# Table matmuls that write every fourth word of a PSUM bank

## The chip, the cores and the metric

The kernel runs on one core of a Trainium2 chip. The metric is the device time of one execution in microseconds. Before the change three runs gave 1797.10, 1792.04 and 1797.41 us, median 1797.1.

## The reference

One layer of a streaming encoder, 512 tokens of 1024 features, all in float32: a chunked attention and an mLSTM with gates, and behind them a layer of very many single-neuron experts (PEER). The change touches the last one:

```
q = (xb @ w_pq).reshape(PEER_BLOCK, PEER_HEADS, 2, D_KEY // 2)
s = jnp.einsum("thpd,hpnd->thpn", q, sub_keys)
s_top, i_top = lax.top_k(s, PEER_TOPK)
...
e = i1 * N_KEYS + i2
gate = jax.nn.softmax(best, axis=-1)
act = jax.nn.gelu(jnp.einsum("thkd,td->thk", u_exp[e], xb))
return jnp.einsum("thk,thkd->td", gate * act, v_exp[e])
```

Every token picks 16 experts for each of 8 heads, 128 in all, out of 128 x 128, by two keys i1 and i2, and each has a gate.

## The kernel before, in words

128 tokens get their experts by gathering rows from HBM. For the other 384 the kernel computes all 16384 experts densely, 128 at a time, and multiplies each activation by a table of gates, which is zero where the token did not pick the expert.

The stages follow each other: mixers and projections up to about 500 us, the selection of experts (`scores`, `select`) to about 700 us, the table build (`build`) from 702 to 868 us, the dense experts (`output`, with the gather of the 128 tokens woven in) to the end. Beside selection and build runs `ahead`, which computes the first 40 of the 128 groups of hidden activations (`hidden`: 24 matmuls into `ps_act`, with the u rows loaded on the SP queue and split by ACT, DVE and POOL into a high and a low part). Its pace beside the build is 0.15 of a group for each step of `build`.

The table of a token t has an entry for every pair (i1, i2). It is the product of two one-hot matrices: `oa` has, for each of the token's 128 slots (partitions), the gate in the column of i2; `o4` has a one in the column of i1, for four tokens at once. One matmul for each token, 128x128 by 128x128 in float32, gives the table (L766); the profile shows each such matmul as two records. Four tokens fill a bank of PSUM (128 partitions x 512 words). ACT then copies the bank into the block `st` in SBUF (L767), which holds 32 tokens as [partition][i1][token]: the 32 tokens of one i1 lie side by side. A block is full after eight banks, and POOL's queue writes it to HBM with one DMA of 2 MB (L772). There are 12 blocks, so 96 banks and 96 copies.

Who makes the operands: DVE `o4` (L750), one per bank; of the four `oa` of a bank, DVE makes two, POOL one (L764), and ACT one by two operations (L760, L761). Banks for `ps_g` come from the tags g and w, two each; `st` has two buffers, so one is filled while the other is written out.

Each engine has a queue of its own and waits on semaphores, which the builder places from the reads and writes of the tiles. The order inside a queue is planned by the builder, which simulates the program's timeline (L1024): the loops issue the 24 matmuls of a group of `ahead` in a row, and the trace shows them interleaved with table matmuls. Behind the stage, `output` loads v rows (`vst`) and table blocks (`gq`) on the SP queue and gathers on POOL's.

The lines of this text: L766 table matmul, L767 copy, L772 block's DMA, L750/760/761/764 operands, L163 to L165 the three matmuls of a split product (`ps_act` in `hidden`, `acc` in `output`), L150 and L153 the split, L135 the loads.

Of the kernel before, what the change touches and what calls it, by code (L numbers as in the profile page):

```python
# [21 lines left out]
P = 128  # L22
# [58 lines left out]
def tile_block(  # L81
# [17 lines left out]
    stop=None,  # L99
):  # L100
    nc = tc.nc
# [8 lines left out]
    def bank(tag, name):  # L110
        return psum.tile([P, 512], F32, tag=tag, name=name, bufs=4 if tag == "acc" else 2)
# [623 lines left out]
    def build(cp, i, slots):  # L735

        ps = bank("g", "ps_slT")
        for j in range(3):
            nc.tensor.transpose(ps[:, j * P : (j + 1) * P], slots[:, j].rearrange("p h k -> p (h k)"), ident)
        sT = cp.tile([P, 3, P], F32, tag="sT", name="sT", bufs=2)  # L740
        nc.scalar.copy(sT, ps[:, : 3 * P].rearrange("p (j t) -> p j t", j=3))
        neg = cp.tile([P, 2, P], F32, tag="neg", name="neg", bufs=2)
        nc.scalar.mul(neg, sT[:, 1:, :], -1.0)
        for b in range(P // TB):
            st = cp.tile([P, P, TB], F32, tag="gst", name="gst", bufs=2)
            for t4 in range(TB // 4):
                ps = bank("gw"[t4 % 2], "ps_g")
                o4 = cp.tile([P, 4, P], F32, tag="two", name="o4", bufs=TWO)
                t0 = b * TB + t4 * 4
                mark = nc.vector.tensor_tensor(  # L750
                    out=o4, in0=iota.unsqueeze(1).broadcast_to([P, 4, P]),
                    in1=sT[:, 0, t0 : t0 + 4].unsqueeze(2).broadcast_to([P, 4, P]), op=ALU.is_equal,
                )
                for tt in range(4):
                    t = b * TB + t4 * 4 + tt
                    oa = cp.tile([P, P], F32, tag="oap" if tt == 1 else "oad", name="oa", bufs=OAP if tt == 1 else OAD)
                    at = sT[:, 1, t : t + 1]
                    gt = sT[:, 2, t : t + 1]
                    if tt == 0 and t4 % ACT_D < ACT_N:
                        nc.scalar.activation(oa, iota, AF.Abs, bias=neg[:, 0, t : t + 1])  # L760
                        nc.scalar.activation(oa, oa, AF.Relu, scale=neg[:, 1, t : t + 1], bias=gt)  # L761
                    else:
                        e = nc.gpsimd if tt == 1 else nc.vector
                        e.tensor_scalar(oa, iota, at, gt, op0=ALU.is_equal, op1=ALU.mult)  # L764
                    ob = o4[:, tt]
                    nc.tensor.matmul(ps[:, tt * P : (tt + 1) * P], oa, ob, start=True, stop=True)  # L766
                nc.scalar.copy(  # L767
                    st[:, :, t4 * 4 : t4 * 4 + 4].rearrange("p i t -> p t i"),
                    ps.rearrange("p (t i) -> p t i", t=4),
                )  # L770
                yield
            nc.gpsimd.dma_start(gd[i * (P // TB) + b], st)  # L772
            state.setdefault("marks", []).append(mark.ins)
# [6 lines left out]
    def front(sp, dp, h2T):  # L780
        yield from scores(sp, h2T)
        for i in range(NG, 4):
            yield from build(dp, i, state["slots"][:, i])
# [244 lines left out]
```

## Time and profile before

| what | before |
|---|---|
| median of three runs | 1797.1 us (1792.04 to 1797.41) |
| profiled execution | 1789.01 us |
| its span, first to last instruction | 1787.2 us |
| PE busy | 1711.7 us (96%) |
| DVE busy | 1372.9 us (77%) |
| ACT busy | 841.5 us (47%) |
| POOL busy | 824.8 us (46%) |
| copies L767, all 96 | 104.8 us, mean 1129 ns |
| table matmuls L766, 768 records | 103.4 us |

PE, DVE, ACT, POOL and SP are the engines; PEld is PE's loading of weights. Times in the views are microseconds from the first instruction, those marked ns excepted. Instructions of one engine overlap at their ends, so that the time from start to start of two in a row tells better than a duration how long one holds the engine. The ends of matmuls are modelled.

### The profile page before, as it was taken

To read this page: it belongs to the slowest core of one execution; us is meant where nothing else is said; L and a number is where in the kernel's file an instruction comes from. 1 tells how busy PE (TensorE), PEld (TensorE's weight loads), DVE (VectorE), ACT (ScalarE), POOL (GpSimd) and SP (SyncE) were. 2 spreads that over 40 slices of the span, in tenths; PEclk is the share of its full clock that TensorE was granted. 3 is DMA by queue.
4 is the path that set the end of the run, shared out by engine and by line. 5 is a ranking of instruction groups with operands and counts; after the bars stand their busy time and mean duration, and the time that the engine had idled before them with its cause. 6 is when DMAs were issued, how large, how long until landed. Compare 5 with 4: busy or idle time off the path is not lost.

```text
span 1787.2 us, 25467 instructions
## 1 busy us (share of the span) xinstructions
PE 1711.7 (96%) x8671; PEld 1483.7 (83%) x8671; DVE 1372.9 (77%) x2868; ACT 841.5 (47%) x1624; POOL 824.8 (46%) x692
## 2 busy tenths in 40 slices
PE   5999999999899988999999999999999999999997
PEld 4766678888798777888889999999999999998886
DVE  7557656674599998788277988989898998898445
ACT  5544545444533326999643343434443334334443
POOL 0000000000267677788446666677766777673221
PEclk9999999999999999999999999999999999999999
DMA  8424234553222333545799999989999989988653
GB/s 298 151 66 142 77 107 141 205 196 118 96 95 89 117 106 126 218 195 212 294 375 322 345 314 353 338 316 340 352 343 342 349 312 356 335 294 294 217 201 106
DMA packets 129940, 413.35 MB, mean 231 GB/s; under 512 B 12049, under 2 KB 38801, under 8 KB 128274
## 3 DMA queue, kind: packets, MB, share of 16 engines
q1 hardware_dynamic: 91218, 252.33, 41.0%
q0 software_dynamic: 38592, 159.40, 23.8%
q8 instruction: 68, 1.11, 0.2%
q14 instruction: 62, 0.51, 0.1%
HBM read 376.03 MB, written 35.66 MB: 230 GB/s over the span
## 4 chain that ended last, share of the span: by engine, by line
PE 79%; DVE 9%; ACT 7%; DMA 2%; issue 2%; POOL 1%; SPq 0%; DVEq 0%; ACTq 0%; POOLq 0%
PE acc L165 10%; PE acc L163 10%; PE acc L164 10%; PE ps_act L165 8%; PE ps_act L163 8%; PE ps_act L164 8%; ACT gst L767 4%; DVE wlo L153 1%; ACT oa L761 1%; PE ps_ya L361 1%; PE ps_s L341 1%; PE ps_pq L165 1%; PE ps_pq L163 1%; PE ps_pq L164 1%; PE ps_qk L163 1%
## 5 line engine op out<-in xcount | busy, mean ns | idle before, releaser
L150 ACT CAST whi<-wst 128x512 fp32r<-128x512 f32 x408 | 253.1, 623 | 479.4 <-PE ps_act L164 277.0
L165 PE MATMUL ps_act<-h2T_hi,wlo 128*128 128x384 f32 x1024 | 347.5, 339 | 7.2 <-DVE wlo L153 6.1
L163 PE MATMUL ps_act<-h2T_hi,whi 128*128 128x384 f32 x1024 | 346.5, 338 | 0.0
L164 PE MATMUL ps_act<-h2T_lo,whi 128*128 128x384 f32 x1024 | 346.1, 338 | 0.0
L164 PE MATMUL acc<-wlo,ehi 128*128 128x512 f32 x768 | 299.1, 391 | 0.0
L163 PE MATMUL acc<-whi,ehi 128*128 128x512 f32 x768 | 293.4, 390 | 5.8 <-ACT whi L150 5.8
L153 DVE TENSOR_TENSOR wlo<-wst,whi 128x512 fp32r<-128x512 f32 x275 | 206.9, 755 | 109.8 <-ACT whi L150 103.8
L165 PE MATMUL acc<-whi,elo 128*128 128x512 f32 x768 | 286.9, 391 | 0.0
L153 POOL TENSOR_TENSOR wlo<-wst,whi 128x512 fp32r<-128x512 f32 x133 | 184.6, 1394 | 192.5 <-ACT whi L150 185.8
L150 ACT CAST whi<-vst 128x512 fp32r<-128x512 f32 x256 | 158.0, 620 | 180.9 <-PE acc L165 143.3
L710 POOL DMA_INDIRECT ur<-in_u_r,ei x128 | 153.6, 1200 | 115.1 <-DVE junk L713 95.2
L153 POOL TENSOR_TENSOR wlo<-vst,whi 128x512 fp32r<-128x512 f32 x85 | 132.9, 1564 | 155.2 <-ACT whi L150 139.8
L724 POOL DMA_INDIRECT vr<-in_v_r,ei x128 | 163.6, 1278 | 86.9 <-DVE sum_v L730 68.7
L165 PEld LDWEIGHTS ps_act<-h2T_hi,wlo 128*128 128x128 f32 x1024 | 193.3, 189 | 10.2 <-DVE wlo L153 8.0
L163 PEld LDWEIGHTS ps_act<-h2T_hi,whi 128*128 128x128 f32 x1024 | 193.4, 189 | 3.8
L164 PEld LDWEIGHTS ps_act<-h2T_lo,whi 128*128 128x128 f32 x1024 | 193.4, 189 | 3.8
L730 DVE SCALAR_TENSOR_TENSOR sum_v<-vr,act,sum_v 128x1024 f32<-128x1024 f32 x127 | 180.3, 1420 | 1.6 <-DMA vr<-in_v_r,ei 0.8
L163 PEld LDWEIGHTS acc<-whi,ehi 128*128 128x128 f32 x768 | 144.5, 188 | 34.3 <-ACT whi L150 6.1
L713 DVE SCALAR_TENSOR_TENSOR junk<-ur,h 128x1024 bf16<-128x1024 f32 x128 | 170.9, 1335 | 0.9
L165 PEld LDWEIGHTS acc<-whi,elo 128*128 128x128 f32 x768 | 144.1, 188 | 30.6 <-DVE elo L841 0.5
L164 PEld LDWEIGHTS acc<-wlo,ehi 128*128 128x128 f32 x768 | 144.1, 188 | 28.4
L153 DVE TENSOR_TENSOR wlo<-vst,whi 128x512 fp32r<-128x512 f32 x171 | 132.5, 776 | 28.1 <-ACT whi L150 27.4
(300 smaller groups left out, 3018.9 us busy)
## 6 DMA issues: line engine op xcount, KB each, us to landing
wst<-in_u_t SPq DMA_DIRECT2D x128, 512.0 KB
vst<-in_v_e SPq DMA_DIRECT2D x128, 512.0 KB
wst<-in_w_pieces SPq DMA_DIRECT2D x76, 512.0 KB
wst<-in_w_ada SPq DMA_DIRECT2D x48, 512.0 KB
gd<-gst POOLq DMA_DIRECT2D x12, 2048.0 KB
gq<-gd SPq DMA_DIRECT2D x16, 1536.0 KB
ad<-gelu SPq DMA_DIRECT2D x8, 768.0 KB
aq<-ad SPq DMA_DIRECT2D x8, 768.0 KB
```

The costliest lines, as they stand in the source:

```text
L150: nc.scalar.copy(hi, t[:, cs])
L153: e.tensor_tensor(out=lo, in0=t[:, cs], in1=hi.bitcast(F32), op=ALU.subtract)
L163: nc.tensor.matmul(o, a[0], b[0], start=first, stop=False)
L164: nc.tensor.matmul(o, a[0], b[1], start=False, stop=False)
L165: return nc.tensor.matmul(o, a[1], b[0], start=False, stop=last)
L341: nc.tensor.matmul(pss[:, :n], qaT[po : po + 64, cs], kaT[po : po + 64, hp, :n], start=True, stop=True)
L361: nc.tensor.matmul(psy[po : po + 64, cs], va[:, kt, h * 64 : (h + 1) * 64], pt[:, kt * P : (kt + 1) * P], start=kt == 0, stop=kt == qt,)
L710: nc.gpsimd.indirect_dma_start(out=t, out_offset=None, in_=u_r, in_offset=bass.IndirectOffsetOnAxis(ap=ei[:, j : j + 1], axis=0))
L713: nc.vector.scalar_tensor_tensor(junk(), t, 1.0, state["h2"][i], op0=ALU.mult, op1=ALU.mult, accum_out=act[:, j : j + 1])
L724: nc.gpsimd.indirect_dma_start(out=t, out_offset=None, in_=v_r, in_offset=bass.IndirectOffsetOnAxis(ap=ei[:, j : j + 1], axis=0))
L730: nc.vector.scalar_tensor_tensor(sum_v, t, act[:, j : j + 1], sum_v, op0=ALU.mult, op1=ALU.add)
L767: nc.scalar.copy(st[:, :, t4 * 4 : t4 * 4 + 4].rearrange("p i t -> p t i"), ps.rearrange("p (t i) -> p t i", t=4),)
```

## The change

The matmul of the tt-th token of a bank no longer writes words 128 tt to 128 tt + 127, but words tt, tt + 4, tt + 8 and so on. So the bank holds [i1][token] in place of [token][i1]. The copy reads its 512 words in order, as it did before. Its writes come in another order: before, 128 single words, 32 words apart, for each token in turn; now runs of four neighbouring words (four tokens of one i1), the runs 32 words apart. What stands in `st` in the end is the same.

```
                     ob = o4[:, tt]
-                    nc.tensor.matmul(ps[:, tt * P : (tt + 1) * P], oa, ob, start=True, stop=True)
+                    nc.tensor.matmul(ps[:, tt::4], oa, ob, start=True, stop=True)
                 nc.scalar.copy(
-                    st[:, :, t4 * 4 : t4 * 4 + 4].rearrange("p i t -> p t i"),
-                    ps.rearrange("p (t i) -> p t i", t=4),
+                    st[:, :, t4 * 4 : t4 * 4 + 4],
+                    ps.rearrange("p (i t) -> p i t", t=4),
                 )
```

## Rows read from the trace of the kernel before

**Rows 1.** The page, first part: busy time, share of the span and instructions of each engine.

```profile
PE 1711.7 (96%) x8671; PEld 1483.7 (83%) x8671; DVE 1372.9 (77%) x2868; ACT 841.5 (47%) x1624; POOL 824.8 (46%) x692
```

**Rows 2.** The page, second part: busy tenths in 40 slices of 44.7 us, DMA engines alike.

```profile
PE   5999999999899988999999999999999999999997
...
ACT  5544545444533326999643343434443334334443
...
DMA  8424234553222333545799999989999989988653
```

**Rows 3.** Windows: stretch, its length, busy us of each engine, clock, DMA share, GB/s.

```profile
702.00:868.00 166.00, 155.91 (x1104) 145.05 (x1104) 127.15 (x288) 164.96 (x323) 132.53 (x124) 1.00 0.52 203
868.00:880.00 12.00, 12.00 (x72) 12.00 (x71) 2.97 (x5) 5.45 (x12) 3.19 (x3) 1.00 1.01 368
880.00:900.00 20.00, 14.22 (x73) 13.61 (x73) 6.45 (x12) 7.13 (x14) 8.59 (x9) 0.83 1.01 366
900.00:1600.00 700.00, 700.00 (x3534) 636.44 (x3533) 614.21 (x768) 278.46 (x506) 473.24 (x359) 1.00 0.93 336
```

**Rows 4.** Chain of waits from 702 to 868 us, summed by line.

```profile
by line: ACT gst L767 43.2%; ACT oa L761 13.1%; ACT oa L760 8.9%; PE ps_g L766 7.2%; ACT whi L150 5.5%; POOL oa L764 4.2%; issue 3.8%; PE ps_act L165 3.0%; PE ps_act L164 2.9%; PE ps_act L163 2.8%; POOL wlo L153 2.7%; ACT gelu L790 2.2%; PE
```

**Rows 5.** Groups by line and shape, 702 to 868 us; columns as in the page's fifth part.

```profile
L767 ACT COPY gst<-ps_g 128x512 f32<-128x512 f32 x96 | 104.8, 1129 | 0.0
L766 PE MATMUL ps_g<-o,oa 128*128 128x128 f32 x768 | 103.4, 281 | 10.1 <-ACT gst L767 4.1 <-ACT oa L761 3.5 <-POOL oa L764 2.2
L764 POOL TENSOR_SCALAR oa<-iota,sT 128x128 f32<-128x128 f32 x94 | 100.1, 1076 | 2.3 <-PE ps_g L766 1.7
...
L163 PE MATMUL ps_act<-h2T_hi,whi 128*128 128x384 f32 x110 | 38.2, 347 | 0.0
```

**Rows 6.** Timeline of ACT from 802.92 us: start, length, instruction.

```profile
802.92 1.14 ACT L767 COPY gst<-ps_g 128x512 f32<-128x512 f32 x1
803.80 0.45 ACT L760 ACTIVATE oa<-iota,neg 128x128 f32<-128x128 f32 x1
804.09 1.10 ACT L767 COPY gst<-ps_g 128x512 f32<-128x512 f32 x1
804.93 0.54 ACT L761 ACTIVATE oa<-oa,sT,neg 128x128 f32<-128x128 f32 x1
```

**Rows 7.** Timeline of ACT at 615.51 us, in the selection stage.

```profile
615.51 0.59 ACT L627 COPY sc<-ps_sc 128x512 f32<-128x512 f32 x1 [0.50 <-PE ps_sc L625]
615.99 0.59 ACT L621 COPY pqT<-ps_pq 128x512 f32<-128x512 f32 x1
```

**Rows 8.** Timeline of PE from 771.00 us, one round of the build stage.

```profile
771.00 1.05 PE L766 MATMUL ps_g<-o,oa 128*128 128x128 f32 x8
771.81 0.42 PE L164 MATMUL ps_act<-h2T_lo,whi 128*128 128x384 f32 x1
772.07 0.34 PE L165 MATMUL ps_act<-h2T_hi,wlo 128*128 128x384 f32 x1
772.24 1.05 PE L766 MATMUL ps_g<-o,oa 128*128 128x128 f32 x8
```

**Rows 9.** Timeline of PE at 1000.22 us, in the expert stage.

```profile
1000.22 0.39 PE L163 MATMUL acc<-whi,ehi 128*128 128x512 f32 x1
1000.45 0.40 PE L164 MATMUL acc<-wlo,ehi 128*128 128x512 f32 x1
```

**Rows 10.** Waits from 702 to 868 us: who waited for whom, total, times, longest.

```profile
PEld ps_g L766 <- ACT gst L767: 9.6, 24, 0.6
...
POOL gd L772 <- ACT gst L767: 6.7, 2, 4.0
```

**Rows 11.** Hand-over: timeline of SP, chain of waits, timeline of PE.

```profile
878.62 0.33 SPq L135 DMA_DIRECT2D wst<-in_u_t  x1
...
879.68 16.25 DMA vst<-in_v_e
...
896.68 1.65 PE L163 MATMUL acc<-whi,ehi 128*128 128x512 f32 x3 [5.78 <-ACT whi L150]
```

## The prediction

> **What bounds the kernel now.** The page's engine line comes first: PE is busy for 96% of the span, nobody else for more than 77% [rows 1]. That is an average over stages, so the slices come next: ACT stands at 2 to 6 tenths nearly everywhere and at 9 only in three slices of 44.7 us, the seventeenth to the nineteenth [rows 2]. They lie in the table build, which the change edits. Cut to its time, 702 to 868 us, the windows show ACT busy for 164.96 of 166 us, PE for 155.91, POOL for 132.53, DVE for 127.15, the DMA engines at 0.52 of their time [rows 3]. The chain of waits of the stretch says the same from the other side: 43.2% of it is the copy of L767, 22.0% the two ACT operations of L760 and L761, 7.2% the table matmuls [rows 4]. So in this stage ACT sets the pace, with the copy as its largest part. In the rest of the span PE does: from 900 to 1600 us it is busy for 700.00 of 700 us [rows 3].
>
> PE's 155.91 us are too many to serve as its need, since the ends of pipelined matmuls are modelled. I take start-to-start times. In a steady stretch one round of eight table records and two ps_act matmuls lasts 772.24 - 771.00 = 1.24 us [rows 8]. Inside it the second ps_act holds PE for 772.24 - 772.07 = 0.17 us; the first ps_act of a round starts early and holds 0.09 us more, so I count both at 0.174 and the eight records at (1.24 - 0.35) / 8 = 0.112 us each. The stage has 768 records (two to each of the 384 matmuls of L766) and 3 x 110 ps_act matmuls [rows 5]. PE's need is 768 x 0.112 + 330 x 0.174 = 86.0 + 57.4 = 143.4, with six small transposes 144 us. That leaves 166 - 144 = 22 us in which PE stands still, in pieces mostly too short for the busy time to show.
>
> **The copy.** The 96 copies stay 96, with the same 512 words each in and out. What changes is the order of the writes: now consecutive words land 32 words apart in the block, afterwards four words lie side by side. Two copies, each with another ACT operation queued right behind it, hold ACT for 803.80 - 802.92 = 0.88 and 804.93 - 804.09 = 0.84 us [rows 6]; I take 0.85. An ordinary copy of 128x512 from PSUM into consecutive words, again with the next one queued, holds it for 615.99 - 615.51 = 0.48 us [rows 7]. The source of both is read in order, so the 0.37 us between them belong to the scattered writes. The trace has no copy with runs of four. Its bounds are 0.48 us (all of the penalty goes) and 0.85 us (none does, because every run still ends in a jump); below 0.48 nothing speaks for it, since the number of words is the same as in the fastest row. I take 0.48, the row nearer in kind: three of four steps are between neighbours. That takes 96 x 0.37 = 35.5 us off ACT, which then needs 165 - 35.5 = 129.5 us of the stage.
>
> **The table matmuls.** Count, operands and array time stay. Each record writes 128 words 16 bytes apart instead of 128 neighbours. No matmul of the trace writes so. A lower bound is 0.112 us, as now; a scattered write can save the array nothing. For the upper bound I borrow the only scattered write that the trace has, that of the copy, which costs 0.85 / 0.48 = 1.77 times the ordered one: 0.112 x 1.77 = 0.198 us. I take 0.112, for this reason: the fp32r matmuls of the later stage write 512 columns every 1000.45 - 1000.22 = 0.23 us, 2.2 columns per ns [rows 9], and the table records only 128 in 0.112 us, 1.14 columns per ns. The write side is asked for half of what it is seen to deliver, so a scattered write may cost up to twice an ordered one before a record becomes longer.
>
> The Trainium skill speaks against this choice: its page "PSUM — Partial Sum Buffer", section "Specifications (TRN2)", says that PSUM's lines hold two fp32 values and that an output pattern that isn't contiguous slows matmuls considerably, without a figure. No row here shows it; by that rule the run goes the way of the first rival below, 1841 us, and by the sentence above it the way of the forecast, 1781 us.
>
> **The sum.** Once ACT needs 129.5 us, PE with 144 is the next in line, then POOL with 132.5 and DVE with 127. The gain cannot be 35.5 us: it ends where PE runs without a gap, 22 us. It will not reach that. ACT alone was 15% above the next engine and reached 99% busy; PE would be only 9% above POOL, and the two feed each other in short steps (one POOL row of L764 per four matmuls, 1.08 us each [rows 5]). Some waits of the stage vanish with the slow copy: the weight load of the records waited 9.6 us for gst in 24 pieces, and POOL stood for 6.7 us at the block's DMA because the last copy was late [rows 10]; while POOL stands there, the next block's rows queue behind it. I take PE at 96% of its time, a stage of 150 us, a gain of 16 us. Nothing is added to any queue; the order of work may be planned anew, because the builder simulates the program, and rows 8 (eight and two in turn, where the loops issue 24 ps_act in a row) show that it does interleave. I count that as part of a spread of the gain from 8 to 22 us.
>
> Behind the stage the gain has to survive. At 880 to 900 us PE stands for 5.78 us, waiting for the first v rows, whose transfer takes from 879.68 for 16.25 us with the DMA engines at 1.01 [rows 3, 11]. That transfer is issued right behind the last u rows, which go out at 878.62 us [rows 11], so it moves forward with the stage. Afterwards PE has no gap for 700 us [rows 3], so an earlier start is an earlier end.
>
> The profiled execution has a span of 1787.2 us and took 1789.0; by the sum it would take 1773. The median of the runs shown is 1797.1, some 8 us above it, and the forecast stands against that: 1797.1 - 16 = **1781 us**.
>
> **Rivals.** *The matmuls pay for the scattered write.* Place: PE in the build stage. For it: PE is already the second engine of the stage, and ACT shows that jumps cost this chip something [rows 6, 7]. Against it: the half rate above [rows 9]. At 0.198 us a record PE needs 768 x 0.198 + 58 = 210 us, the stage grows by 44 us, and the run takes 1841 us. It decides from the point where PE's need passes the 166 us of today: (166 - 58) / 768 = 0.141 us a record, 26% over now. *Half of it.* At 0.123 to 0.165 us PE needs 152 to 185 us; the result lies between 8 us faster, with some waits left, and 19 us slower: 1789 to 1816 us. *The copy gets no faster.* If each jump counts and not its length, runs of four might still hold ACT for 0.85 us: ACT stays the bound, 1797 us. That the change doesn't do what it says is this case. Against it is that three jumps of four disappear. *The gain is given back at the hand-over.* The DMA engines are full from 868 to 900 us; if the v rows could not come sooner, PE would only wait longer than 5.78 us: 1797 us. Against it is the share of 0.52 in the stage [rows 3], which leaves room for what has to be moved before.
>
> **How the numbers follow.** The forecast has 0.58, the rival of the slow matmuls 0.18, its half form 0.11, the copy that stays slow 0.08, the hand-over 0.05. The forecast's own range is 1770 to 1789 us: a gain of 8 to 22 us, and 5 us more at the lower end because the runs shown begin at 1792 us. The range for 8 in 10 reaches to 1815 us, over the copy, the hand-over and the half form; outside are the slow matmuls and 0.02 below. A change of under 0.3%, 5.4 us, cannot be told from none. Faster: 0.55 of the forecast and 0.04 of the half form, 0.59. The same: 0.07 of the slow copy, 0.04 of the hand-over, 0.03 of the forecast, 0.02 of the half form, 0.16. Slower: the slow matmuls with 0.18, 0.05 of the half form, 0.02 of the two cases without an effect, 0.25.
>
> **What would show it.** The copy's row: mean near 0.6 us in place of 1.13, start to start near 0.48. The record's: a round of eight and two still 1.24 us. The build stage 14 to 22 us shorter, its chain led by PE and no longer by L767, ACT at 8 to 9 tenths. The 5.78 us wait before the first acc matmul unchanged. The prediction is wrong if a record takes more than 0.14 us start to start, or if a copy still holds ACT for more than 0.7 us: then ACT saves under 15 us, and with ACT still ahead of PE the gain is smaller than that.

## The result, and the profile after

Four runs gave a median of 1768.0 us (1767.1 to 1768.8) against 1795.6 us for the kernel before (1792.0 to 1797.4, four runs). The ratio is 0.9865, interval 0.9847 to 0.9883: of the 1789.0 us of the profiled execution before, 24 us less, between 21 and 27. The profiled execution of the changed kernel took 1767.1 us, span 1765.3, which is 21.9 us less than before. The forecast was 16 us.

The page of the changed kernel: the line of the engines, and the slices of PE and ACT.

```profile
PE 1705.3 (97%) x8671; PEld 1486.5 (84%) x8671; DVE 1380.5 (78%) x2868; ACT 806.3 (46%) x1624; POOL 832.6 (47%) x692
...
PE   5999999999999897999999999999999999999997
...
ACT  4544545443543334998533443433434443434443
```

ACT has given back 35 us of busy time (841.5 to 806.3), as much as the forecast took off it; of its three nines of [rows 2] two are left, over a shorter stage. Where the gain lies is read from the copies: the view of L767 gives the start of the first and of the last. First before, then after (columns: least, median and greatest length in ns, then the two starts).

```profile
L767 ACT COPY gst<-ps_g x96: 1017/1114/1327, 704.5 to 866.9; 128x512 f32<-128x512 f32 x96
```

```profile
L767 ACT COPY gst<-ps_g x96: 565/586/630, 706.5 to 846.4; 128x512 f32<-128x512 f32 x96
```

162.4 us have become 139.9. The first copy starts 2.0 us later than before, and from the last copy to the end it is 918.9 us instead of 920.3: 2.0 - 22.5 - 1.4 = -21.9 us. So the stage's 22.5 us are the whole gain. The windows of the changed kernel, with the stage in the first line (columns as in [rows 3]):

```profile
704.00:848.50 144.50, 144.13 (x1102) 143.64 (x1102) 133.68 (x289) 131.17 (x324) 136.48 (x125) 1.00 0.61 236
...
861.00:881.00 20.00, 16.73 (x83) 15.67 (x83) 8.79 (x16) 8.05 (x16) 9.65 (x9) 0.91 0.99 368
900.00:1580.00 680.00, 680.00 (x3439) 619.02 (x3438) 602.65 (x747) 272.45 (x494) 467.84 (x352) 1.00 0.93 335
```

PE is busy for 144.13 of 144.50 us, where it was for 155.91 of 166 [rows 3]; ACT for 131.17, where it was full. Since the ends of matmuls are modelled, the starts are the better measure: between the first and the last table matmul lie 768 records and 309 ps_act matmuls, at 0.112 and 0.174 us 139.8 us of work, and the stretch takes 141.3 us, where it took 162.4 before. The chain of waits of the stage has changed hands:

```profile
by line: PE ps_g L766 48.0%; PE ps_act L163 11.1%; PE ps_act L164 11.0%; PE ps_act L165 11.0%; POOL oa L764 8.1%; DMA gd<-gst 6.2%; POOL wlo L153 1.7%; issue 1.5%; PE ps_slT L739 0.5%; POOL gd L772 0.4%; ACT oa L760 0.3%; ACT oa L761 0.3%; 
```

In [rows 4] the copy held 43.2% and the table matmuls 7.2%; now these hold 48.0%, the ps_act matmuls 33.1%, and L767 doesn't appear. The two lines of the change, by group, answer to [rows 5]:

```profile
L766 PE MATMUL ps_g<-o,oa 128*128 128x128 f32 x768 | 94.6, 275 | 0.4 <-ACT oa L761 0.4
...
L767 ACT COPY gst<-ps_g 128x512 f32<-128x512 f32 x96 | 56.1, 590 | 11.5 <-DMA gd<-gst 6.2 <-PE ps_g L766 5.3
```

The copy's mean has gone from 1129 to 590 ns. How long it holds ACT is read from two starts in a row, as in [rows 6]; the timeline of ACT:

```profile
721.99 0.61 ACT L767 COPY gst<-ps_g 128x512 f32<-128x512 f32 x1
722.45 0.45 ACT L760 ACTIVATE oa<-iota,neg 128x128 f32<-128x128 f32 x1
```

722.45 - 721.99 = 0.46 us, against 0.84 to 0.88 before and 0.48 for the copy into consecutive words [rows 7]. A round of PE, as in [rows 8]:

```profile
760.25 1.05 PE L766 MATMUL ps_g<-o,oa 128*128 128x128 f32 x8
761.05 0.42 PE L165 MATMUL ps_act<-h2T_hi,wlo 128*128 128x384 f32 x1
761.31 0.34 PE L163 MATMUL ps_act<-h2T_hi,whi 128*128 128x384 f32 x1
761.49 1.05 PE L766 MATMUL ps_g<-o,oa 128*128 128x128 f32 x8
```

761.49 - 760.25 = 1.24 us, to the hundredth what it was: the scattered matmuls cost nothing here. Two waits of the stage:

```profile
POOL gd L772 <- ACT gst L767: 6.9, 3, 3.4
ACT gst L767 <- DMA gd<-gst: 6.2, 4, 2.4
```

The first was there before, with 6.7 us [rows 10]; the prediction let it vanish with the slow copy, and it didn't. With it POOL, busy for 136.48 us, has 143.4 of the 144.5 us taken, nearly as much as PE. The second is new: at four places the copies fill a block before the DMA has emptied the other one. It is 6.2% of the chain, but PE's work leaves only 1.5 us of its stretch free. The last view is the hand-over, chain and PE, as in [rows 11]:

```profile
860.51 13.74 DMA vst<-in_v_e
```

```profile
875.00 1.46 PE L163 MATMUL acc<-whi,ehi 128*128 128x512 f32 x3 [3.27 <-ACT whi L150]
```

PE stands for 3.27 us instead of 5.78. The stage's gain reached the end of the run.

### The profile page after: what moved, and what is told of

Its sections match the earlier page's. It is cut to its first block, busy times and chain, and to the rows that moved or that the text cites. A ratio compares the mean times of both kernels' runs of the same rounds, so it can differ in the third digit from the quotient of the medians.

```text
span 1765.3 us, 25467 instructions
## 1 busy us (share of the span) xinstructions
PE 1705.3 (97%) x8671; PEld 1486.5 (84%) x8671; DVE 1380.5 (78%) x2868; ACT 806.3 (46%) x1624; POOL 832.6 (47%) x692
## 4 chain that ended last, share of the span: by engine, by line
PE 80%; DVE 13%; DMA 4%; issue 1%; POOL 1%; ACT 1%; SPq 0%; DVEq 0%; ACTq 0%
PE acc L165 10%; PE acc L164 10%; PE acc L163 10%; PE ps_act L165 8%; PE ps_act L163 8%; PE ps_act L164 8%; PE ps_g L766 4%; DVE wlo L153 2%; DMA wst<-in_w_ada 1%; PE ps_ya L361 1%; PE ps_s L341 1%; PE ps_qk L163 1%; DVE i L648 1%; PE ps_qk L165 1%; DVE sc L649 1%
## 5 line engine op out<-in xcount | busy, mean ns | idle before, releaser
L153 DVE TENSOR_TENSOR wlo<-wst,whi 128x512 fp32r<-128x512 f32 x275 | 207.0, 756 | 98.2 <-ACT whi L150 91.1
L153 POOL TENSOR_TENSOR wlo<-wst,whi 128x512 fp32r<-128x512 f32 x133 | 184.4, 1393 | 180.9 <-ACT whi L150 174.9
L724 POOL DMA_INDIRECT vr<-in_v_r,ei x128 | 168.6, 1317 | 84.5 <-DVE sum_v L730 65.9
L153 POOL TENSOR_TENSOR wlo<-vst,whi 128x512 fp32r<-128x512 f32 x85 | 131.0, 1541 | 151.7 <-ACT whi L150 136.1
L471 POOL TENSOR_SCALAR_AFFINE_SELECT mbd<-mbc 128x512 f32<-128x512 f32 x4 | 4.7, 1163 | 319.5 <-ACT mbc L469 319.5
```

The lines of the kernel that those rows point to most:

```text
L153: e.tensor_tensor(out=lo, in0=t[:, cs], in1=hi.bitcast(F32), op=ALU.subtract)
L724: nc.gpsimd.indirect_dma_start(out=t, out_offset=None, in_=v_r, in_offset=bass.IndirectOffsetOnAxis(ap=ei[:, j : j + 1], axis=0))
```

## Experiments

The theory: the copy was dear by the order of its writes alone; ACT's sum of work bounded the stage; PE's sum bounds it now. Code is shortened: a pattern in quotes stands for the tile's rearrange. All comparisons are with runs of the kernel before on the same chip.

**One half of the change at a time.** The first kernel has the matmuls of the change and the copy's old order (against the changed kernel):

```
 matmul(ps[:, tt::4], oa, ob, ...)
-copy(st[:, :, t4 * 4 : t4 * 4 + 4], ps "p (i t) -> p i t")
+copy(st[...] "p i t -> p t i", ps "p (i t) -> p t i")
```

> The matmuls write every fourth word as in the changed kernel, but the copy writes as before, single words 32 apart, token by token; it therefore reads every fourth word of the bank. Theory (the order of the copy's writes is the whole price, the scattered matmul costs nothing): the copy holds ACT for about 0.85 us again, a table record 0.112 us, ACT is the bound of the build stage, which is back at about 164 us, and the time is within 4 us of the kernel before. Rival (the layout of the bank is what helps, the copy gains by reading it so): the copy is near 0.47 us and the time near that of the changed kernel, some 24 us below before. Third possibility: reading every fourth word costs something of its own; then the copy goes above 0.85 us, by 96 x the excess slower than before.

Ratio 1.0012, interval 0.9998 to 1.0025 (median 1793.9 against 1789.7 us): no gain. Timeline of its ACT:

```profile
721.85 1.08 ACT L767 COPY gst<-ps_g 128x512 f32<-128x512 f32 x1
722.69 0.42 ACT L760 ACTIVATE oa<-iota,neg 128x128 f32<-128x128 f32 x1
```

722.69 - 721.85 = 0.84 us, as before, although the copy now reads every fourth word of the bank: these reads cost nothing. On the scattered matmul this run says little, since ACT sets the pace and PE has time to spare.

The second has the old matmuls and the new order of the copy (against the kernel before):

```
 matmul(ps[:, tt * P : (tt + 1) * P], oa, ob, ...)
-copy(st[...] "p i t -> p t i", ps "p (t i) -> p t i")
+copy(st[:, :, t4 * 4 : t4 * 4 + 4], ps "p (t i) -> p i t")
```

> The matmuls write as before, 128 words in a row for each token; the copy writes runs of four as in the changed kernel and so reads the bank with steps of 128 words. Theory: only the writes count, the copy holds ACT for about 0.47 us, the build stage lasts about 141 us, and the time is that of the changed kernel, about 24 us below before (ratio 0.986). Rival (reads out of order cost as much as writes do): the copy stays at 0.8 us or more and the time within 4 us of before. Between them: a copy of about 0.6 us would still leave ACT, at 142 us, level with PE's 144, so that nearly the whole gain would stay.

Ratio 0.9860, interval 0.9834 to 0.9885: the whole gain. Timeline of its ACT:

```profile
722.18 0.60 ACT L767 COPY gst<-ps_g 128x512 f32<-128x512 f32 x1
722.65 0.44 ACT L760 ACTIVATE oa<-iota,neg 128x128 f32<-128x128 f32 x1
```

722.65 - 722.18 = 0.47 us, with reads that step by 128 words. Its stage, with all matmuls writing in a row:

```profile
L767 ACT COPY gst<-ps_g x96: 565/586/622, 706.7 to 846.4; 128x512 f32<-128x512 f32 x96
```

139.7 us from the first start to the last, against 139.9 with scattered matmuls: where PE has no time to spare, the scattering of 384 matmuls makes a difference of 0.2 us. So the edit of the matmul, on which the prediction spent its first rival, was not needed: the gain sits in the order in which the copy writes to SBUF.

**How many neighbours.** The changed kernel with runs of two: `st[...] "p i (a t) -> p a i t"`, t = 2, and the bank read alike.

> As the changed kernel, but the copy writes runs of two words: 256 jumps in place of 128 (changed) or 512 (before). Theory A, each jump has one price: between 0.85 us with 512 and 0.465 us with 128 jumps that is 1.0 ns a jump, so 0.59 us a copy. Theory B, a word is dear only when no neighbour follows it: 0.465 us as with runs of four. ACT needs 141 us by A and 129 us by B, both under PE's 144, so the time is about that of the changed kernel by either (A may lose up to 5 us by ACT and PE being level); the copy's start-to-start time tells them apart.

Ratio 0.9870, interval 0.9844 to 0.9896, level with the change. Its ACT:

```profile
724.38 0.66 ACT L767 COPY gst<-ps_g 128x512 f32<-128x512 f32 x1
724.87 0.46 ACT L760 ACTIVATE oa<-iota,neg 128x128 f32<-128x128 f32 x1
```

It holds ACT for 724.87 - 724.38 = 0.49 us. Of 0.38 us between single words and runs of four, pairs give back 0.35. A price for each jump (0.59 us) is refuted, and "a word is dear only without a neighbour" is nearly right. The Trainium skill, page "SBUF — State Buffer", section "Specifications (TRN2)", says that a line has 16 bytes and that full bandwidth needs at least two accesses to a line; this run agrees, within 0.03 us a copy.

**What a scattered matmul costs at full rate.** The prediction took the scattered writes for free because a table record asks for half of the columns per ns that PE is seen to deliver. 128 bf16 matmuls behind the last one test this, in one execution; their result is not used.

```
shapes = [(pr, pb), (pr "p (i t) -> p t i", pb ...), (pr "p (i a t) -> p a i t", pb ...), (pr, pb)]
for po, rhs in shapes: 32 x matmul(po, pb[:, :P], rhs)
```

> The changed kernel with 128 extra matmuls behind the last one, bf16, 128x128 by 128x512, whose result nobody reads: 32 that write 512 words in a row, 32 that write them four words apart in four passes over the bank, 32 in pairs of two, 32 in a row again. They ask the write side for about 2.2 columns per ns, twice what a table record asks for. The reason given in the prediction (a scattered write is free at half rate and may cost up to twice at full rate): the ordered ones take about 0.22 us start to start, those four apart more than that, up to 0.45 us. Rival (a scattered write costs nothing at any rate): all four groups alike, 0.22 us. If the pairs are at 0.22 us and the single words above, two neighbours are enough.

Windows of 6 us in the first, second and third group, of these instructions alone (busy time of PE and of the loading of weights, with counts):

```profile
1759.00:1765.00 6.00, 6.00 (x29) 2.73 (x28) 1.00 0.43 165
1767.00:1773.00 6.00, 6.00 (x15) 1.95 (x14) 1.00 0.05 18
...
1780.00:1786.00 6.00, 6.00 (x30) 2.73 (x28) 1.00 0.00 0
```

In the same time 28 weight loads (one to a matmul) for words in a row, 14 for words four apart, 28 for pairs. Start to start the medians are 0.216, 0.429 and 0.216 us, at a granted clock of 1.00: a scattered write costs twice an ordered one at full rate, to within 1%, and a pair nothing. That fits the reason of the prediction: scattered writes still take 512 / 0.429 = 1.19 columns per ns, and a table record asks for 1.14. It is not shown on fp32 matmuls, which might write in another way; none here asks for more. The page "PSUM — Partial Sum Buffer" of the Trainium skill (section "Specifications (TRN2)"), by which an output pattern that isn't contiguous slows matmuls, agrees with the single words at 512 columns of bf16; the pairs, and the fp32 table records, whose round kept its 1.24 us, were not slowed, and there the measurement decides.

**Less work for ACT by another way.** Instead of a faster copy, ACT makes an operand only for every other bank, DVE the other 48: `ACT_N, ACT_D = 2, 2` becomes `1, 2`, first in the kernel before, then in the changed one. The builder plans the order of work anew for both.

> The kernel before, with its slow copy, but ACT makes an operand only for every other bank; DVE makes the other 48. That takes 48 x (0.385 + 0.29) = 32 us off ACT in the build stage and puts 48 x 0.26 = 12 us on DVE (127 to 139 us busy). Theory (only ACT's load counted, and PE with its 144 us takes over): the stage shrinks from 164 to about 143 us and the run gains 20 to 24 us, as much as the change, without touching the copy. Rival (the slow copy costs by its length in the round trip bank, copy, bank, not by ACT's load): the copy keeps its 0.85 us and the gain stays under 8 us. Another: DVE becomes the bound; then the stage is about 150 us and the gain 14 us.

Ratio 0.9920, interval 0.9903 to 0.9937: 14 us, with the slow copy. The stage in one window:

```profile
708.00:855.00 147.00, 139.58 (x1044) 135.00 (x1043) 134.99 (x328) 135.82 (x225) 137.40 (x121) 1.00 0.54 212
```

It shrank from about 164 to 146 us between the first copy and the end of the last. That the copy's own length is what matters is refuted: it still holds ACT for 0.86 us. But PE is not full: DVE, ACT and POOL are all at 135 to 137 us. The gain is that of the third expectation, though not by its cause, DVE. POOL is the one without a pause: besides its 137.40 us it stands at the block's DMA until the last copy is done,

```profile
POOL gd L772 <- ACT gst L767: 9.0, 3, 4.8
```

together 146.4 of 147 us, and its rows of L764 and L153 are 36% of the chain. The new plan also left 39 ps_act matmuls fewer between the first and the last table matmul (270, not 309).

> The changed kernel with the same shift of 48 operands from ACT to DVE. Theory (PE bounds the stage, ACT is free for 15% of it): no gain, within 3 us of the changed kernel; ACT's busy time in the stage falls from 131 to about 100 us and changes nothing. If DVE at 139 to 146 us comes level with PE, it may lose up to 4 us. Rival (ACT still sets the pace somewhere in the stage): a further gain of 4 us or more.

Ratio 0.9908, interval 0.9891 to 0.9924: 5 to 8 us above the change (by the medians, 1773.6 to 1768.0, and by the ratios), and the intervals lie apart. The stage, and the longest wait of PE's weight loads in it:

```profile
701.00:842.00 141.00, 136.21 (x1035) 133.46 (x1034) 134.95 (x326) 102.81 (x224) 136.78 (x119) 1.00 0.56 220
```

```profile
PEld ps_g L766 <- POOL oa L764: 7.0, 11, 1.6
```

ACT is down to 102.81 us, and nothing is gained: it was no longer the bound. The stage itself has not grown:

```profile
L767 ACT COPY gst<-ps_g x96: 563/585/623, 701.3 to 841.4; 128x512 f32<-128x512 f32 x96
```

```profile
POOL gd L772 <- ACT gst L767: 3.3, 2, 1.9
```

140.1 us from the first start to the last, as in the changed kernel (139.9), although PE has 39 ps_act matmuls less to do in it here too. POOL holds it there, with 136.78 and 3.3 of 141 us. The matmuls left out come behind the stage, 39 x 0.174 = 6.8 us, which is about the loss. So, as far as this kernel tells, PE and POOL end the gain of the change at nearly the same place.

**How close may the next engine come.** The mis-sized step was that PE, with ACT and POOL near, would lose 4% to gaps. The first try gave ACT 11 us more by copying every fourth bank twice (`if t4 % 4 == 0:` a second `copy` behind the first).

> The changed kernel with the copy of every fourth bank done twice: 24 x 0.465 = 11 us more for ACT, which then needs about 141 us, 2% under PE's 144. It tests the step of the prediction that was mis-sized: that an engine 9% above the next one loses 4% of its time to gaps. By that step ACT this close must cost PE several per cent: 6 us or more above the changed kernel. By the other view (four banks and the operands' buffers take up the short waits, and only the largest sum counts): within 3 us of the changed kernel.

Ratio 1.0009, interval 0.9999 to 1.0019: the whole gain is gone, more than either side expected. The windows, and the copies:

```profile
704.00:752.00 48.00, 48.00 (x367) 48.00 (x366) 45.20 (x92) 44.57 (x108) 43.81 (x41) 1.00 0.58 226
752.00:800.00 48.00, 48.00 (x353) 47.97 (x351) 42.99 (x92) 44.67 (x110) 45.24 (x39) 1.00 0.58 216
...
880.00:900.00 20.00, 4.33 (x15) 3.50 (x13) 9.46 (x16) 1.24 (x2) 12.98 (x10) 0.66 1.04 396
```

```profile
L767 ACT COPY gst<-ps_g x96: 566/597/674, 706.9 to 860.5; 128x512 f32<-128x512 f32 x96
```

PE is full to 800 us and nearly so to 848 (46.79 of 48). The last copy still comes 14 us later than in the changed kernel, because the extra copies made the builder plan another order: 365 instead of 309 ps_act matmuls stand between the first and the last table matmul, 56 x 0.174 = 9.7 us more for PE. That is work done earlier, not lost. Most of what is lost comes at 880 to 900 us, where PE is busy for 4.33 us and waits for the first v rows:

```profile
PE acc L163 <- ACT whi L150: 14.2, 1, 14.2
```

In that order, besides, six gathers of u rows stand on POOL's queue ahead of the last block's DMA (issued at 865.83 us; 847.32 in the changed kernel). The next kernel lets the gathers wait for that DMA:

```
-state.setdefault("marks", []).append(mark.ins)
+state.setdefault("marks", []).append(sent.ins)     # sent: the block's dma_start
```

> The kernel with every fourth bank's copy done twice lost 24 us, nearly all behind the build stage: the plan had put six gathers of u rows on POOL's queue ahead of the last block's DMA, the table blocks and v rows came late, and PE stood for 14 us. Here the gathers wait until the last block's DMA is issued. If that order was the cause, the wait of PE for the first v rows falls to 3 to 6 us and the run comes down by 10 us or more, to within 12 us of the changed kernel. If ACT's extra 11 us were the cause, the run stays near 1791 us.

Ratio 0.9980, interval 0.9968 to 0.9993, 5 us better than without, but half of what was expected (its runs spread from 1780 to 1793 us, and the profiled one is the fastest), and the wait stayed:

```profile
PE acc L163 <- ACT whi L150: 12.8, 1, 12.8
```

So the order on POOL's queue was a part only. The chain of this kernel shows what PE waits for, and the waits of the SP queue, first without and then with the change to the gathers, show the same in both:

```profile
858.74 9.59 DMA gd<-gst
868.58 21.80 DMA gq<-gd
```

```profile
SPq L828 <- DMA gd<-gst: 7.9, 1, 7.9
```

```profile
SPq L828 <- DMA gd<-gst: 6.9, 1, 6.9
```

The load of the first table block (`gq`) stands on the SP queue ahead of the v rows and waits there for the last block's DMA, so a late last copy holds up the v rows too. In the changed kernel the queue has no such wait. Behind it the first transfers are slow: 21.34 us for the v rows without the change to the gathers and 21.80 us for the table block with it, where the first v rows of the changed kernel took 13.74. A kernel that puts the v rows ahead was not run.

The second try keeps the order of work: the copy of every fourth, or second, bank writes in the old order (`out4` and `in4` are its output and input).

```
+if t4 % 4 == 0:        # slow_half: t4 % 2 == 0
+    out4, in4 = (a.rearrange("p i t -> p t i") for a in (out4, in4))
 nc.scalar.copy(out4, in4)
```

> The changed kernel with the order of work kept, but the copy of every fourth bank writes as before, single words: 24 x (0.85 - 0.465) = 9 us more for ACT, which needs about 139 us then, 4% under PE's 144. By the prediction's step (an engine 9% above the next one loses 4% of its time) ACT this close costs 6 us or more over the changed kernel. By the view that short waits are taken up by the buffers and only the largest sum counts: within 3 us of the changed kernel, with PE busy for over 99% of the stage.

Ratio 0.9866, interval 0.9841 to 0.9890: the same as the change. The window, which holds the whole stage, and the copies:

```profile
704.00:852.00 148.00, 147.62 (x1124) 147.16 (x1123) 137.94 (x296) 142.28 (x331) 138.84 (x127) 1.00 0.60 232
```

```profile
L770 ACT COPY gst<-ps_g x96: 569/609/1162, 709.1 to 849.1; 128x512 f32<-128x512 f32 x96
```

PE 147.62 of 148 us with ACT at 142.28. Within 4% of PE, ACT costs it nothing.

> The same with every second bank: 48 x 0.385 = 18 us more, ACT needs about 148 us, 3% over PE. By the largest sum the stage is 4 to 6 us longer than in the changed kernel (from 140.5 us between the first and the last copy to some 145 or 147), and the run with it; before the change, with 165 us for ACT, it is 23 us. By the prediction's step, two engines level, it is 8 us or more.

Ratio 0.9889, interval 0.9863 to 0.9916, 1773.0 us: 4 to 5 us above the change; the intervals overlap, so the stage has to tell, again by window and copies.

```profile
704.00:852.00 148.00, 146.24 (x1099) 143.48 (x1098) 132.93 (x288) 146.94 (x323) 134.33 (x124) 1.00 0.59 228
```

```profile
L770 ACT COPY gst<-ps_g x96: 557/942/1279, 706.2 to 851.0; 128x512 f32<-128x512 f32 x96
```

Now ACT is full (146.94) and PE has gaps (146.24, by modelled ends). From the first copy to the end of the last it is 145.5 us, against 140.5 in the changed kernel and 163.6 before. With ACT needing 130, 139, 148 and 165 us the stage takes 140.5, 140.5, 145.5 and 163.6: the larger of PE's sum and ACT's, to within 4 us, and no loss where these two come near.

**Less work for PE.** The table operands in fp32r, so that a table matmul is one record; the gates of the dense experts are rounded by it. Matmuls write in a row, the copy runs of four: `F32` becomes `F32R` in the tiles `o4` and `oa`.

> Matmuls write in order and the copy writes runs of four, but the table's two operands are fp32r, so that each table matmul is one record instead of two; the gates of the dense experts are rounded to fp32r by it. PE's need in the stage falls by 384 x 0.112 = 43 us to about 101 us, if a record stays at 0.112 us or less. Theory (the largest engine's sum sets the stage): the next are DVE (134 us busy), POOL (136) and ACT (131), so the stage ends at about 135 to 140 us and the run gains 4 to 9 us over the changed kernel, not 43. But the u groups that run beside the build are paced by the order of work, so PE time freed here is used only if these groups move up. Rival: PE is the only thing that counts, and the run gains 30 us or more.

Ratio 0.9991, interval 0.9981 to 1.0000: no gain at all.

```profile
704.00:752.00 48.00, 44.43 (x288) 43.27 (x287) 48.00 (x78) 42.42 (x104) 47.54 (x43) 1.00 0.60 221
752.00:800.00 48.00, 45.67 (x297) 45.42 (x297) 46.49 (x85) 43.55 (x106) 42.52 (x38) 1.00 0.68 254
800.00:848.00 48.00, 39.49 (x146) 33.52 (x146) 46.07 (x122) 41.47 (x105) 43.06 (x39) 0.53 0.54 214
...
880.00:900.00 20.00, 4.00 (x11) 3.49 (x12) 11.16 (x22) 2.60 (x6) 10.54 (x8) 0.61 1.04 395
```

```profile
PE acc L163 <- ACT whi L150: 12.5, 1, 12.5
PE ps_g L766 <- DVE oa L764: 6.0, 6, 2.1
```

DVE is full (48.00 of 48) or nearly, as expected, so PE's saved records cannot be used. Three things went beyond that. The stage takes 150.9 us from the first copy to the end of the last, not 135 to 140; this plan, too, has 365 ps_act matmuls in it, with their splits on DVE and POOL, and whether that is all stays open. In the last of three windows of 48 us, from 800 to 848 us, the granted clock is 0.53, nearly all of the time the lower level of 1.2 GHz: this order has used up the ps_act matmuls earlier (175, 190 and 0 in the three windows), and PE stood between table matmuls for their operands. And at 880 to 900 us PE shows the same stand as above, 12.5 us for the first v rows, again under an order planned anew and with the SP queue waiting 5.1 us for the last block's DMA.

## Why the prediction was right, and which step was mis-sized

**The bound.** Right. ACT's load set the stage: 35 us less by fast copies, or 18 of them given back by slow ones, move the stage as the larger sum says, and the kernel with half the operands moved to DVE gains without touching the copy.

**The copy.** Right: 0.46 us, expected 0.48; 96 x 0.39 = 37 us off ACT, expected 35.5. Its reason, neighbours in place of jumps, is shown by the runs of two. That the reads don't matter was assumed and is shown by both half changes.

**The table matmuls.** Right in size (0.112 us kept), and its reason (half rate hides a price of two) fits the bf16 matmuls, with 1.19 columns per ns delivered and 1.14 asked for: the margin was 4%. The first rival names a price that exists, but in other matmuls. That the upper bound borrowed from ACT, 1.77 times, came near the 1.99 found at full rate is luck: it was another engine and another memory.

**The step that was mis-sized** is "I take PE at 96% of its time, a stage of 150 us, a gain of 16 us". PE's work filled 139.8 of 141.3 us, 99%, and the stage gave 22.5 us, its upper bound. I had read the waits of the stage before, in which everything hung on ACT, as if an engine 9% below the next would cause such waits too. The kernel with every fourth copy slow shows that one 4% below doesn't. A likely reason is that work waits in four banks and in the buffers of the operands, and that the ps_act matmuls, which need nothing of the table, stand between the table matmuls; no run changed either. The step was also wrong on POOL: its stand at the block's DMA didn't vanish (6.7 and 6.9 us), and with it POOL is level with PE, not 9% below.

**The hand-over.** Right in that the v rows moved forward (879.68 to 860.51 us) and the gain survived; the wait, forecast unchanged, got shorter, 5.78 to 3.27 us. The hand-over rival did not come true, and the change itself left the order on every engine as it was. Under a new plan the place is weak: three of the five kernels whose work was planned anew waited 12.5 to 14.2 us exactly there. The prediction counted a new plan as a small part of its spread; the runs show up to 24 us under one.

**The sum.** Median 27.6 us lower, by the ratio 24, in the profile 21.9; the range's lower end, 1770 us, was worked out for a gain of 22 us. The measured median lies 2 us below it; by the ratio, 1797.1 x 0.9865 = 1773 us, the result is inside, near that end. The mechanism was right, and the gain was put too low.

## What to carry to other kernels

When one engine stands at 99% in a stage, work out every other engine's need from start-to-start times, and add what its queue stands for at a DMA; the gain of relieving the first ends at the largest of the others, and here, under an unchanged order of work, it went all the way there. Look at how an engine writes before changing who writes what: here the order of one copy's writes was worth 24 us and the layout of the bank nothing. Where the builder plans the order, compare the order of both kernels before believing that a difference of time belongs to the edit.

## What the runs showed that was not expected

ACT writes 512 single words to SBUF in 0.84 to 0.88 us, pairs in 0.49 and runs of four in 0.46. The step with which it reads PSUM changed neither end (1 or 4 words with single writes, 1 or 128 with runs of four): a pair already escapes the price. In bf16 matmuls PE writes 512 scattered words to PSUM in 0.429 us and pairs in 0.216 us, as fast as words in a row. In both cases two neighbours are what counts.
